# First expert pair's activations ahead of the place gates, residual rebuild behind them, in a one-core decoder layer

## The chip, the cores and the metric

The kernel runs on one core of one Trainium2 chip. The metric is the device time of one execution in microseconds (us); the profile is one execution taken by the hardware profiler. The engines are named as in the profile: PE (matmul), PEld (its weight loads), DVE (VectorE), ACT (ScalarE), POOL (GpSimd), SP (the queue that issues most loads).

## The reference

One decoder layer over 512 tokens of width 1024: a token mixer (sparse attention and a gated DeltaNet), a LayerNorm, and a hierarchical mixture of experts with a second LayerNorm. The change is in the last part. Cut to it:

```python
h = x * (1.0 + sc2) + sh2                      # 512 tokens x 1024
# each token: one of 4 groups, in it the top 2 of 8 experts, with gates
def expert_block(args):                        # 32 experts, FF = 512
    xb, e = args
    hb = jax.nn.silu(xb @ w_gate[e]) * (xb @ w_up[e])
    return hb @ w_down[e]
y = sum over a token's experts of gate * expert_block(token)
x = layer_norm(alpha * x + (1.0 + gt2) * y, ln_g[1], ln_b[1])
```

## The kernel before

The experts are worked in 16 pairs (`pair(p)`, `PAIRS = 16`), four experts to a group. A pair's tokens are gathered with one-hot matmuls into 2 x 64 places. PE then computes for the pair `pwg` (gate product) and `pwu` (up product), each as two halves of 16 matmuls (`first_product(p, "wg" or "wu", i)`, L1259). `expert_rows` (L1139) makes the activations: tanh on ACT (L1142), a multiply on DVE (L1143, both in a tile `eth` that has one buffer), and the product with `pwu` on DVE (L1145, tile `hb`). `turned_rows` (L1149) transposes `hb` on PE (L1153, `hbT`) and copies it on ACT (L1155, `hbTs`). `last_products` (L1271) multiplies by the down weights (`py`, L1279), and `weighted` (L1158) scales the result by the gate (DVE L1162, tile `ys` with two buffers) and splits it in two parts (ACT L1167, DVE L1168). One pair later `combine_block` (L1176) puts them back to token order (PE `comb`, L1184) and DVE adds them to the residual rows `acc` (L1190).

Which place holds which token and with what gate is worked out once per two pairs by `place_gates` (PE `gs` L1229, then ACT L1231, whose rows share the one-buffer tile `eth`) and `turned_gates` (PE `gsT` L1240, then small DVE steps L1243 and L1246 into `gsl`). `token_hots` (L1250, DVE L1253) makes the one-hot rows for `comb`; `tokens_of` (DVE L975) those for the gather of a later group.

Between the routing and pair 0 the residual rows `acc` are rebuilt from the two parts of the normed tokens: eight DVE additions (L1519), each 128 x 512, and behind each one POOL addition (L1527) of a bias row `b_row`, which POOL loads (L1522) and scales (L1523). `b_row` stands in the two `ys` buffers. The two halves of `acc` lie in memory that early loaded weights used (`acc0`, `acc1` in `EARLY`), so their rebuild waits for the matmuls that read these weights.

Each engine runs its instructions in one order that is fixed when the program is built: by the order of writing, by what is ready, and by explicit edges. `tc.issue_after(ins)` puts what its block issues on the engine of `ins` behind `ins`. `in_turn()` (L1299) chains PE's pieces of the pairs in this way. `begun` is the last matmul of pair 0's `pwu`; behind it come `gs` and `gsT`. In `whole(p)` (L1318) the call `rows_of(p)` stands ahead of the pair's remaining PE work.

Weights come as 1 MB loads on SP (L1108, `load`), in one chain, each into a slot that a matmul some 13 loads before has released. Ahead of pair 14 there is a loop over overflowing places (`overflow`, L1428), which all engines enter together.

Of the kernel before, what the change touches and what calls it, by code (L numbers as in the profile page):

```python
# [9 lines left out]
F32 = mybir.dt.float32  # L10
# [4 lines left out]
OP = mybir.AluOpType  # L15
# [65 lines left out]
def decoder_layer(ctx: ExitStack, tc: tile.TileContext, A, out, dbg=None):  # L81
    nc = tc.nc
    v, g, s, pe = nc.vector, nc.gpsimd, nc.scalar, nc.tensor
# [110 lines left out]
    for c in (slice(0, 512), slice(512, 1024)):  # L194
        o = pmm("c")
        pe.matmul(o, row1, crow[:, c], start=True, stop=True)
        th = dp.tile([P, S], F32, name="cth", tag="cacc", bufs=2)
# [77 lines left out]
    def project(n, i, rhs=None, name="pj", split=None, bank=None, first=0):  # L275

        hi, lo = split or take(n, i)
        o = (bank or pmm)(name)[:, first:]
        r = rhs or (h_hi, h_lo)
        for k in range(KT):  # L280
            mm3(o, (hi[:, k, :], lo[:, k, :]), (r[0][:, k, first:], r[1][:, k, first:]), k == 0, k == KT - 1)
        look_ahead()
        return o
# [56 lines left out]
    first = {i: project("w_in", i, split=early[i], bank=banks[i]) for i in range(6)}  # L340
# [130 lines left out]
    for h in range(H):  # L471
# [5 lines left out]
        for n in range(NT):  # L477
            v.scalar_tensor_tensor(NTm[:, h, n, :], o[:, n, :], per_head(brk2, n, h), et[:, n, :],
                                   op0=OP.mult, op1=OP.mult)
# [11 lines left out]
    for j in range(31):  # L491
        n, w = 31 - j, j + 1
# [40 lines left out]
    for j in range(4):  # L533
        o = project("w_in", T_QI + j, first=P)
        for b in range(2):
            r, x = slice(64 * b, 64 * b + 64), slice(64 - 64 * b, 128 - 64 * b)
            s.activation(q_st[b][r, j, :], o[r], AF.Copy)
            v.tensor_tensor(q_st[b][x, j, :], o[r], q_st[b][r, j, :].bitcast(F32), op=OP.subtract)
    for i in range(1, NT):
        N = (i + 1) * P  # L540
        sc = isc[i - 1]
        for h in range(H):
# [9 lines left out]
            else:  # L552
                v.scalar_tensor_tensor(sc[:, :N], rl[:, :N], widx[:, i, h:h + 1], sc[:, :N],
                                       op0=OP.mult, op1=OP.add)
# [73 lines left out]
    for h in range(H):  # L628
# [32 lines left out]
        for n in range(NT):  # L661
            v.scalar_tensor_tensor(qk[:, n, :], o[:, n, :], per_head(rk, n, h), et[:, n, :],
                                   op0=OP.mult, op1=OP.mult)
# [3 lines left out]
                                          op=OP.mult)  # L667
# [195 lines left out]
    for d in range(KT):  # L863
# [14 lines left out]
        for t in range(NT):  # L878
            x = part[0][:, t * P:(t + 1) * P]
# [138 lines left out]
    n = slice(0, 512)  # L1018
# [117 lines left out]
    load_ahead([seq[i] for i in FIRST])  # L1136


    def expert_rows(pg, pu, n):  # L1139

        th = mo.tile([P, FF], F32, name="eth", bufs=1)
        s.activation(th[:n], pg[:n], AF.Tanh, scale=0.5)  # L1142
        v.scalar_tensor_tensor(th[:n], th[:n], 1.0, pg[:n], op0=OP.add, op1=OP.mult)  # L1143
        hb = m2.tile([P, 4, P], F32, name="hb", bufs=1)
        v.scalar_tensor_tensor(hb[:n], th[:n].rearrange("s (p j) -> s j p", j=4), 0.5,  # L1145
                               pu[:n].rearrange("s (p j) -> s j p", j=4), op0=OP.mult, op1=OP.mult)
        return hb

    def turned_rows(hb, n, last=False):  # L1149

        o = pc("hbT", (P, 4, P))
        for j in range(4):
            pe.transpose(o[:, j, :n], hb[:n, j, :], ident[:n, :n])  # L1153
        hT = lp.tile([P, 4, P], F32, name="O") if last else m2.tile([P, 4, P], F32, name="hbTs")
        s.activation(hT[:, :, :n], o[:, :, :n], AF.Copy)  # L1155
        return hT
# [40 lines left out]
    def gather(O, n, xg, j, bank=pb):  # L1197
        o = bank("gx", (P, 2, 256))
        for i in range(2):
            for t in range(NT):  # L1200
                for q, hh in enumerate((n_hi, n_lo)):
                    pe.matmul(o[:, i, :n], hh[:, t, (j + i) * P:(j + i + 1) * P], O[:, t, :n],  # L1202
                              start=(t == 0 and q == 0), stop=(t == NT - 1 and q == 1))
        evacuate(xg, o, j, n, bank is pmm)
# [20 lines left out]
    def place_gates(gi, O):  # L1225

        o = pb("gs", (9, 2 * P))
        for t in range(NT):
            pe.matmul(o, gate_hl[:, t, gi], O[:, t, :], start=(t == 0), stop=(t == NT - 1))  # L1229
        rows = mo.tile([P, FF], F32, name="eth", bufs=1)[:9, :2 * P]  # L1230
        s.activation(rows, o, AF.Copy)  # L1231
        return rows

    def turned_gates(rows):


        o = pb("gsT", (P, 2, 9))
        r = []
        for c in range(2):
            pe.transpose(o[:, c, :], rows[:, c * P:c * P + P], ident[:9, :9])  # L1240
        for c in range(2):
            gs = mo.tile([P, 9], F32, name="gsl", bufs=4)
            v.scalar_tensor_tensor(gs[:, 1:], o[:, c, 8:9].to_broadcast([P, 8]), float(SLOTS), lim, op0=OP.add, op1=OP.subtract)  # L1243
            for x in range(2):
                p = slice(64 * x, 64 * x + 64)
                v.tensor_reduce(gs[p, 0:1], o[p, c, 4 * c + 2 * x:4 * c + 2 * x + 2], axis=X, op=OP.add)  # L1246
            r.append(gs)
        return r
# [5 lines left out]
                        gs_of[p][:, 1:, None].to_broadcast([P, 8, SLOTS]), op=OP.is_equal)  # L1254
        return OT

    groups, first, OTs, py_done = {}, {}, {}, [None]

    def first_product(p, nm, i):  # L1259

        if i == 0:
            first[p, nm] = pmm("p" + nm)
        o, xg, c0 = first[p, nm], groups[p // 2][1], p % 2 * P
        ws = [half(A["w_gate" if nm == "wg" else "w_up"], 2 * p + x, i, nm) for x in range(2)]
        for j in range(4):
            for x in range(2):
                done = pe.matmul(o[64 * x:64 * x + 64], xg[:, 4 * i + j, c0 + 64 * x:c0 + 64 * x + 64],  # L1267
                                 ws[x][:, j * FF:(j + 1) * FF], start=(i == 0 and j == 0), stop=(i == 1 and j == 3))
        return done
# [28 lines left out]
    @contextmanager  # L1298
    def in_turn():  # L1299

        with tc.issue_after(behind[0]) if behind[0] is not None else nullcontext():
            yield
        behind[0] = next(i for i in reversed(nc.cur_bb.bb.instructions) if i.engine == begun.ins.engine)

    def rows_of(p):
        return expert_rows(first.pop((p, "wg")), first.pop((p, "wu")), P)
# [3 lines left out]
    def combinations():  # L1310

        def step(parts, c, OT, t):
            return lambda: combine_block(parts, c, OT, P, t, pa if t % 2 else pb)
        steps = [step(*x, t) for x in waiting for t in range(NT)]
        waiting.clear()
        return steps

    def whole(p):  # L1318


        gi = p // 2
        hb = rows_of(p)
        nxt = groups.get(gi + 1)

        turned = []

        def gates():
            turned.append(place_gates(gi, groups[gi][0]))

        def turn_gates():  # L1330
            gs_of[p], gs_of[p + 1] = turned_gates(turned[0])

        js = () if nxt is None or p == 0 else (0, 2, 4, 6) if p == 1 else (4 * (p % 2), 4 * (p % 2) + 2)
        gathers = [lambda j=j: gather(nxt[0], 256, nxt[1], j, pmm) for j in js]
        combs = combinations()
        gates, turn_gates = ([gates], [turn_gates]) if gi and p % 2 == 0 else ([], [])
        steps = combs[:4] + gates + gathers[:1] + combs[4:] + turn_gates + gathers[1:]
        for f in steps:
            with in_turn():
                f()  # L1340
        with in_turn():
            return turned_rows(hb, P)

    def pair(p):

        gi, q = p // 2, p + 1
        if p == 0:
            with in_turn():
                first_product(q, "wg", 0)
        hT = whole(p)  # L1350
        if p % 2 == 1 and gi + 2 < E // 4 or p == 0:
            n = gi + 2 if p else 1
            groups[n] = tokens_of(n)
        OTs[p] = token_hots(p)
        with in_turn():
            if p:
                first_product(q, "wg", 0)
            first_product(q, "wg", 1)
        with in_turn():
            waiting.extend(y + (OTs[p],) for y in last_products(p, hT))  # L1360
        with in_turn():
            first_product(q, "wu", 0)
            first_product(q, "wu", 1)
# [57 lines left out]
    def overflow():  # L1421
# [6 lines left out]
        with tc.For_i(0, n_over, 1) as it:  # L1428
# [20 lines left out]
            for src in (A["w_gate"], A["w_up"]):  # L1449
                o = pa("pwx")  # L1450
                for i in range(2):
                    w_ = half_of(wx, src, e, i)
                    for j in range(4):
                        pe.matmul(o[:SLOTS], xg[:, 4 * i + j, :SLOTS], w_[:, j * FF:(j + 1) * FF],
                                  start=(i == 0 and j == 0), stop=(i == 1 and j == 3))
                pgu.append(o)
            hT = turned_rows(expert_rows(pgu[0], pgu[1], SLOTS), SLOTS)
            py = [pa("py") for _ in range(2)]
            for i in range(2):
# [48 lines left out]
    started = first_product(0, "wu", 0)  # L1508
    places, turn = m1.tile([P, 2048], F32R, name="places", tag="a0"), [1]
    begun = first_product(0, "wu", 1)  # L1510
    with tc.issue_after(begun.ins):
        gs_of[0], gs_of[1] = turned_gates(place_gates(0, groups[0][0]))

    acc = Parts(*[lp.tile([P, 2, D], F32, name="acc", tag=f"acc{i}", bufs=1) for i in range(2)])
    for c in range(2):
        for t in range(NT):
            x, hi, lo = (y[:, t, :].rearrange(f"q ({o}) -> q j p", j=KT)[:, :, 64 * c:64 * c + 64]
                         for y, o in ((acc, "p j"), (n_hi, "j p"), (n_lo, "j p")))
            v.tensor_tensor(x, hi.bitcast(F32), lo.bitcast(F32), op=OP.add)  # L1519
    b_row = [m2.tile([P, 512], F32, name="ys", bufs=2) for _ in range(2)]  # L1520
    for c in range(2):
        g.dma_start(b_row[c], A["ln"][0][1][c * 512:(c + 1) * 512][None].to_broadcast([P, 512]))  # L1522
# [1 line left out]
    for c in range(2):  # L1524
        for t in range(NT):
            x = acc[:, t, c * 512:(c + 1) * 512]
# [23 lines left out]
    with tc.issue_after(nm_done.ins):  # L1550
        x = acc[:, 0, :]
        s.activation(x, x, AF.Identity, bias=nm[:, 0:1], scale=rs[:, 0:1])
        for t in (1, 2, 3):
            x = acc[:, t, :]
# [4 lines left out]
        x = acc[:, 0, :]  # L1559
# [82 lines left out]
```

## Time and profile before

| | us |
|---|---|
| median of 3 runs | 1273.54 (1272.57 to 1275.81) |
| profiled execution, own time | 1277.16 |
| its span | 1275.5 |
| mean granted TensorE clock of the span | 0.976 |

The page gives the busy time of each engine, the span in 40 slices of 31.9 us with the granted clock (PEclk, tenths of full speed) and the load rate, the chain that ended last, and groups of instructions. A timeline row gives start, duration, engine, line, operation, out<-in and count; in brackets the engine's idle time before it and what ended it.

### The profile page before, as it was taken

The numbers are of one execution on the slowest core, as the hardware profiler recorded it, in microseconds if no ns is written. First come the engines' busy times: TensorE is split into PE (matmuls) and PEld (weight loads), VectorE is DVE, ScalarE is ACT, GpSimd is POOL, SyncE is SP. The second block draws the span as 40 slices with busy tenths as digits, with TensorE's granted clock in tenths as the row PEclk, the third lists the DMA queues.
The fourth block names the chain that finished last, engine by engine and source line by source line (L and its number), as shares of the span: only waits on it lengthen the run. The fifth ranks groups of instructions, "written<-read, shape, count | busy, mean of one in ns | idle before, by whom it ended". The sixth has DMA issues, their size and how long they took to land. (4 is left out here: it accounts for less than half of the span.)

```text
span 1275.5 us, 16286 instructions
## 1 busy us (share of the span) xinstructions
PE 1174.5 (92%) x6042; PEld 803.4 (63%) x6042; DVE 789.2 (62%) x1701; ACT 433.4 (34%) x913; POOL 230.7 (18%) x190
## 2 busy tenths in 40 slices
PE   4977988998899999999999978999999999999994
PEld 2766766777677777778888864454455555555432
DVE  6797898598995656866646876533324243333338
ACT  3454643666455656432223222111111111111102
POOL 4322234233232321000024232300000000000003
PEclk9999998999999999999999989899999999999987
DMA  7614314111211111356644777779999999999792
GB/s 276 254 67 131 109 50 139 56 49 48 67 49 35 67 67 67 128 208 240 248 149 182 291 281 274 292 323 420 422 420 422 421 421 420 421 420 421 318 386 110
DMA packets 75860, 292.37 MB, mean 229 GB/s; under 512 B 19169, under 2 KB 31617, under 8 KB 51202
## 3 DMA queue, kind: packets, MB, share of 16 engines
q1 hardware_dynamic: 58706, 282.47, 56.4%
q10 hardware_dynamic: 16352, 6.16, 2.0%
q0 software_dynamic: 720, 2.66, 0.6%
q8 instruction: 49, 0.80, 0.3%
q14 instruction: 33, 0.27, 0.1%
HBM read 287.57 MB, written 3.70 MB: 228 GB/s over the span
## 5 line engine op out<-in xcount | busy, mean ns | idle before, releaser
L228 PE MATMUL pj<-h_hi,w_hi 128*128 128x512 f32 (+1 forms) x504 | 203.3, 410 | 18.2 <-ACT h_hi L323 12.9
L230 PE MATMUL pj<-h_hi,w_lo 128*128 128x512 f32 (+1 forms) x504 | 204.9, 408 | 4.6 <-POOL w_lo L224 4.0
L229 PE MATMUL pj<-h_lo,w_hi 128*128 128x512 f32 (+1 forms) x504 | 204.9, 407 | 0.0
L224 POOL TENSOR_TENSOR w_lo<-wr,w_hi 128x1024 fp32r<-128x1024 f32 x43 | 108.8, 2534 | 209.2 <-ACT w_hi L223 170.8
L223 ACT ACTIVATE w_hi<-wr 128x1024 fp32r<-128x1024 f32 x85 | 89.7, 1057 | 136.5 <-PE pj L229 92.9
L228 PEld LDWEIGHTS pj<-h_hi,w_hi 128*128 128x128 f32 x504 | 97.2, 193 | 39.7 <-ACT h_hi L323 14.9
L1267 PE MATMUL pwg<-wg,xg 128*64 128x512 f32 x512 | 119.7, 615 | 0.0
L1267 PE MATMUL pwu<-wu,xg 128*64 128x512 f32 x512 | 115.2, 592 | 0.0
L230 PEld LDWEIGHTS pj<-h_hi,w_lo 128*128 128x128 f32 x504 | 97.2, 193 | 24.6 <-POOL w_lo L224 6.1
L229 PEld LDWEIGHTS pj<-h_lo,w_hi 128*128 128x128 f32 x504 | 97.3, 193 | 18.2 <-DVE h_lo L324 0.8
L1279 PE MATMUL py<-wd,hbTs 128*64 128x512 f32 x480 | 106.1, 593 | 0.0
L1267 PEld LDWEIGHTS pwu<-wu,xg 128*64 128x64 f32 x512 | 47.3, 137 | 62.3 <-issue 60.0
L1188 POOL TENSOR_TENSOR acc<-acc,ad 128x256 f32<-128x256 f32 x8 | 6.0, 775 | 442.9 <-PE comb L1184 439.8
L1190 DVE TENSOR_TENSOR acc<-acc,comb 128x512 f32<-128x512 f32 (+1 forms) x128 | 77.6, 663 | 12.8 <-PE comb L1184 12.3
L1143 DVE SCALAR_TENSOR_TENSOR eth<-eth,pwg 128x512 f32<-128x512 f32 x16 | 11.0, 688 | 115.3 <-ACT eth L1142 113.0
L1267 PEld LDWEIGHTS pwg<-wg,xg 128*64 128x64 f32 x512 | 37.9, 141 | 69.2 <-issue 66.7
L1279 PEld LDWEIGHTS py<-wd,hbTs 128*64 128x64 f32 x480 | 39.9, 137 | 63.6 <-issue 63.6
L1162 DVE SCALAR_TENSOR_TENSOR ys<-py,gsl,gt2r 128x512 f32<-128x512 f32 (+1 forms) x34 | 24.4, 718 | 83.2 <-PE py L1279 79.7
L224 DVE TENSOR_TENSOR w_lo<-wr,w_hi 128x1024 fp32r<-128x1024 f32 x42 | 56.8, 1354 | 29.6 <-ACT w_hi L223 28.8
L357 DVE SCALAR_TENSOR_TENSOR cacc<-pad,convw,cacc 128x512 f32<-128x512 f32 x72 | 68.4, 955 | 6.3 <-ACT cacc L355 6.1
L965 ACT ACTIVATE xg<-gx,h2c 128x256 f32<-128x256 f32 x32 | 17.9, 565 | 122.6 <-PE gx L1202 114.8
L1145 DVE SCALAR_TENSOR_TENSOR hb<-eth,pwu 128x512 f32<-128x512 f32 x16 | 17.2, 1077 | 65.8 <-PE pwu L1267 65.8
(476 smaller groups left out, 2340.3 us busy)
## 6 DMA issues: line engine op xcount, KB each, us to landing
wg<-in_w_gate_dram SPq DMA_DIRECT2D x64, 1024.0 KB, 11.7
wu<-in_w_up_dram SPq DMA_DIRECT2D x64, 1024.0 KB, 15.5
wd<-in_w_down_dram SPq DMA_DIRECT2D x60, 1024.0 KB, 12.0
wr<-in_w_in_dram SPq DMA_DIRECT2D x31, 1024.0 KB, 5.0
wada<-in_w_ada_dram SPq DMA_DIRECT2D x23, 1024.0 KB, 5.5
wr<-in_w_br_dram SPq DMA_DIRECT2D x8, 1024.0 KB, 6.4
gr<-g_rows ACTq DMA_DIRECT2D x16, 256.0 KB, 5.0
wr<-in_w_out_dram SPq DMA_DIRECT2D x4, 1024.0 KB, 5.0
```

The costliest lines, as they stand in the source:

```text
L223: s.activation(hi, raw, AF.Copy)
L224: (lo_eng.pop() if len(lo_eng) > 1 else lo_eng[0]).tensor_tensor(lo, raw, hi.bitcast(F32), op=OP.subtract)
L228: pe.matmul(o, a[0], b[0], start=start, stop=False)
L229: pe.matmul(o, a[0], b[1], start=False, stop=False)
L230: pe.matmul(o, a[1], b[0], start=False, stop=stop)
L357: v.scalar_tensor_tensor(acc, pad[:, i:i + S], convw[:, ct, i:i + 1], acc, op0=OP.mult, op1=OP.add)
L965: x = s.activation(xg[:, j, :n], o[:, 0, :n], AF.Identity, bias=h2c[:, 1, 1, j:j + 1], scale=h2c[:, 1, 0, j:j + 1])
L1145: v.scalar_tensor_tensor(hb[:n], th[:n].rearrange("s (p j) -> s j p", j=4), 0.5, pu[:n].rearrange("s (p j) -> s j p", j=4), op0=OP.mult, o ...
L1162: v.scalar_tensor_tensor(ys[:n, :w], py, gs, gt2r[:n, c], op0=OP.mult, op1=OP.mult)
L1190: v.tensor_tensor(acc[:, t, c], acc[:, t, c], o[:, :w], op=OP.add)
L1267: done = pe.matmul(o[64 * x:64 * x + 64], xg[:, 4 * i + j, c0 + 64 * x:c0 + 64 * x + 64], ws[x][:, j * FF:(j + 1) * FF], start=(i == 0 and ...
L1279: pe.matmul(py[c][64 * x:64 * x + 64], hT[:, 2 * i + j, 64 * x:64 * x + 64], ws[x][:, j, 512 * c:512 * c + 512], start=(i == 0 and j == 0) ...
```

## The change

`expert_rows` records its last DVE instruction (L1145) as `rows_done[0]`. Pair 0's `expert_rows` is called right behind `begun` and its result kept in `hidden[0]`, which `whole(0)` takes in place of a call of its own. The place gates of pairs 0 and 1 are then issued behind `begun` (on PE) and behind that L1145 (on DVE), and the eight DVE additions of the residual rebuild (L1519) behind the same L1145. No instruction is added or taken away.

```diff
+    rows_done = [None]
+
     def expert_rows(pg, pu, n):
         th = mo.tile([P, FF], F32, name="eth", bufs=1)
         s.activation(th[:n], pg[:n], AF.Tanh, scale=0.5)
         v.scalar_tensor_tensor(th[:n], th[:n], 1.0, pg[:n], op0=OP.add, op1=OP.mult)
         hb = m2.tile([P, 4, P], F32, name="hb", bufs=1)
-        v.scalar_tensor_tensor(hb[:n], th[:n].rearrange("s (p j) -> s j p", j=4), 0.5,
-                               pu[:n].rearrange("s (p j) -> s j p", j=4), op0=OP.mult, op1=OP.mult)
+        rows_done[0] = v.scalar_tensor_tensor(hb[:n], th[:n].rearrange("s (p j) -> s j p", j=4), 0.5,
+                                              pu[:n].rearrange("s (p j) -> s j p", j=4), op0=OP.mult, op1=OP.mult)
         return hb
...
-    groups, first, OTs, py_done = {}, {}, {}, [None]
+    groups, first, OTs, py_done, hidden = {}, {}, {}, [None], {}
...
         gi = p // 2
-        hb = rows_of(p)
+        hb = hidden.pop(p) if p in hidden else rows_of(p)
...
     begun = first_product(0, "wu", 1)
-    with tc.issue_after(begun.ins):
+    hidden[0] = rows_of(0)
+    with tc.issue_after(begun.ins), tc.issue_after(rows_done[0].ins):
         gs_of[0], gs_of[1] = turned_gates(place_gates(0, groups[0][0]))
...
-            v.tensor_tensor(x, hi.bitcast(F32), lo.bitcast(F32), op=OP.add)
+            with tc.issue_after(rows_done[0].ins):
+                v.tensor_tensor(x, hi.bitcast(F32), lo.bitcast(F32), op=OP.add)
```

## Rows read from the trace of the kernel before

**Rows 1.** From the page: the span, and the load rate in the 40 slices of 31.9 us.

```profile
span 1275.5 us, 16286 instructions
...
GB/s 276 254 67 131 109 50 139 56 49 48 67 49 35 67 67 67 128 208 240 248 149 182 291 281 274 292 323 420 422 420 422 421 421 420 421 420 421 318 386 110
```

**Rows 2.** The waits of PE from 790 us to the end: who waited for whom, us in total, times, longest.

```profile
PE hbT L1153 <- DVE hb L1145: 5.6, 1, 5.6
PE gsT L1240 <- ACT eth L1231: 3.2, 2, 2.8
PE gs L1229 <- DVEq L1428: 2.7, 1, 2.7
PE py L1289 <- ACT O L1155: 0.7, 1, 0.7
```

**Rows 3.** Timeline of PE around the stretch, to pair 1.

```profile
785.85 2.31 PE L1267 MATMUL pwg<-wg,xg 128*64 128x512 f32 x9
787.74 3.85 PE L1267 MATMUL pwu<-wu,xg 128*64 128x512 f32 x16
791.52 0.63 PE L1229 MATMUL gs<-O,gate_hl 128*9 128x256 f32 x4
792.61 0.29 PE L1240 MATMUL gsT<-ident,eth 9*128 9x9 f32 x2 [0.46 <-ACT eth L1231]
798.48 1.11 PE L1153 MATMUL hbT<-ident,hb 128*128 128x128 f32 x4 [5.58 <-DVE hb L1145]
799.53 5.87 PE L1267 MATMUL pwg<-wg,xg 128*64 128x512 f32 x16
805.23 7.03 PE L1279 MATMUL py<-wd,hbTs 128*64 128x512 f32 x32
812.10 7.03 PE L1267 MATMUL pwu<-wu,xg 128*64 128x512 f32 x32
...
819.24 0.50 PE L1184 MATMUL comb<-yh,places 128*128 128x512 f32 x1
```

**Rows 4.** Timeline of DVE, then of ACT, over the same stretch.

```profile
794.12 2.00 DVE L1519 TENSOR_TENSOR acc<-n_hi,n_lo 128x512 f32<-128x512 f32 x2
...
796.76 0.68 DVE L1253 TENSOR_TENSOR places<-slot_no,gsl 128x512 fp32r<-128x512 f32 x1
797.36 1.06 DVE L1145 SCALAR_TENSOR_TENSOR hb<-eth,pwu 128x512 f32<-128x512 f32 x1
798.34 2.06 DVE L975 TENSOR_TENSOR O<-slot_no,pos 128x256 fp32r<-128x256 f32 x4
...
811.52 1.65 DVE L1162 SCALAR_TENSOR_TENSOR ys<-py,gsl,gt2r 128x512 f32<-128x512 f32 x2 [4.73 <-PE py L1279]
...
819.21 1.07 DVE L1145 SCALAR_TENSOR_TENSOR hb<-eth,pwu 128x512 f32<-128x512 f32 x1 [4.65 <-PE pwu L1267]
...
792.19 0.37 ACT L1231 ACTIVATE eth<-gs 9x256 f32<-9x256 f32 x1 [12.40 <-PE gs L1229]
793.00 0.60 ACT L1142 ACTIVATE eth<-pwg 128x512 f32<-128x512 f32 x1 [0.44 <-PE gsT L1240]
```

**Rows 5.** PE after two other short idle times, and the granted clock (the figure behind the POOL column, 1.00 is full) in stretches behind them and in the stretch of the change.

```profile
748.53 0.19 PE L1004 MATMUL pos<-selb,upper_b 128*128 128x32 bf16 x1 [1.88 <-DVE selb L1002]
...
770.35 0.19 PE L1004 MATMUL pos<-selb,upper_b 128*128 128x32 bf16 x1 [1.38 <-DVE selb L1002]
...
750.00:752.00 2.00, 2.00 (x11) 2.00 (x11) 0.69 (x1) 0.00 (x0) 0.00 (x0) 0.50 0.81 340
...
772.00:774.00 2.00, 1.99 (x14) 1.15 (x14) 1.00 (x2) 1.02 (x2) 0.00 (x0) 1.00 0.86 360
...
798.00:800.00 2.00, 1.52 (x6) 1.01 (x8) 2.00 (x5) 0.37 (x1) 2.00 (x2) 0.50 0.00 0
...
804.00:806.00 2.00, 2.00 (x12) 0.65 (x10) 0.00 (x0) 0.53 (x1) 2.00 (x3) 0.99 0.03 8
```

**Rows 6.** Timeline of POOL, and the durations (ns, least/median/most) of the rebuild's additions and of one-hot rows for the gather.

```profile
795.37 1.97 POOL L1523 TENSOR_SCALAR ys<-ys 128x512 f32<-128x512 f32 x1 [2.37 <-DMA ys<-in_ln_dram]
797.43 1.27 POOL L1527 TENSOR_TENSOR acc<-acc,ys 128x512 f32<-128x512 f32 x1
798.66 1.67 POOL L1523 TENSOR_SCALAR ys<-ys 128x512 f32<-128x512 f32 x1
800.30 9.20 POOL L1527 TENSOR_TENSOR acc<-acc,ys 128x512 f32<-128x512 f32 x7
...
L1519 DVE TENSOR_TENSOR acc<-n_hi,n_lo x8: 1081/1093/1123, 786.6 to 795.0; 128x512 f32<-128x512 f32 x8
L1527 POOL TENSOR_TENSOR acc<-acc,ys x8: 1262/1272/1825, 797.4 to 808.2; 128x512 f32<-128x512 f32 x8
...
L975 DVE TENSOR_TENSOR places<-slot_no,pos x4: 417/423/425, 786.2 to 791.0; 128x256 fp32r<-128x256 f32 x4
```

**Rows 7.** The weight loads: SP's issues at 805 us, then the last four loads of `wu` ahead of the loop and the time from issue to landing of these four, and the PE row that uses them.

```profile
805.42 4.24 SPq L1108 DMA_DIRECT2D wd<-in_w_down_dram  x4
...
L1108 SPq DMA_DIRECT2D wu<-in_w_up_dram x4: 327/328/385, 1169.1 to 1176.3; - x4
...
DMA to landing us min/median/max: 19.0/19.6/19.8
...
1197.39 7.09 PE L1267 MATMUL pwu<-wu,xg 128*64 128x512 f32 x32
```

## The prediction

> **What bounds the kernel now.** I read the page first, for where the end is set; then PE's waits in the expert part, since PE has the most work there; then the timelines of PE, DVE, ACT and POOL around the edited lines; then the granted clock; last the loads. The load rate stands near 420 GB/s from slice 28 on [rows 1], so the weights are a candidate for the bound, but in the list of PE's waits from 790 us to the end no row names a DMA [rows 2]. There PE sets the pace, and only four waits are left. The longest, 5.6 us, is the one that the edit touches: pair 0's `hbT` waits for `hb` from DVE [rows 2].
>
> The reader is to see in the PE timeline that `pwu` of pair 0 ends at 787.74 + 3.85 = 791.59, that `gs` and `gsT` fill little, and that `hbT` starts only at 798.48 [rows 3]. The cause stands in the DVE and ACT rows: ACT may start the tanh only at 793.00, since `eth` has one buffer and holds the gate rows until `gsT` has read them; DVE does two rebuild additions from 794.12, then L1143, then one-hot rows (L1253) at 796.76, and only at 797.36 the product L1145 that PE waits for [rows 4]. A second cost follows: the granted clock is 0.50, the lower level of 1.2 GHz, from 798 to 804 us, and full again after it [rows 5], so `hbT` and 16 matmuls of `pwg` take from 798.48 to 805.23 [rows 3].
>
> **The change part by part.** *Activations first.* Nothing is added; the same tanh, multiply and product move up. The tanh needs only pair 0's `pwg`. The last row of `pwg` matmuls before the rest of `pwu` ends at 785.85 + 2.31 = 788.16, whichever product they belong to [rows 3]; tanh (0.60) and L1143 (0.7, taken as the 0.68 of the like-sized L1253) then end by 789.5 [rows 4], under the `pwu` matmuls that run to 791.59, and ACT had been idle 12.40 us there [rows 4]. Without that cover they would cost 1.3 us. So DVE has only L1145 left when `pwu` ends. In pair 1 it starts 0.08 us behind `pwu` (812.10 + 7.03 = 819.13 to 819.21) and takes 1.07 [rows 3, 4]: `hb` is there at 791.59 + 0.08 + 1.07 = 792.74. PE followed `hb` by 0.06 before (798.42 to 798.48) [rows 3, 4], so `hbT` can start at 792.80, 5.7 us earlier.
>
> *Gates behind it.* `gs` stays where it is on PE. Its ACT copy (0.37 [rows 4]) now waits for the one `eth` buffer, thus for L1145: 792.74 to 793.15, and `gsT` (0.29 [rows 3]) can go at 793.2. If PE's order has `hbT` first, `gsT` lies behind it and takes 0.29 off the gain: 5.4. If `gsT` stands first, `hbT` starts at 793.5: 5.0. I take 5.3. Queued behind the later gate rows are `gsl`, the one-hot rows and, by 804 us, the weighting of `py` on DVE; that has 10 us.
>
> *The clock.* PE's idle time becomes 0.65 us (from the end of `gs` at 792.15 to 792.80), or 1.05 with `gsT` first. Behind an idle time of 1.38 us the clock stayed full, behind one of 1.88 us it fell to 0.50 [rows 5]. The new one is below the shorter. At full clock 16 such matmuls take half of 812.10 - 805.23, 3.43, and `hbT` half of 1.05, 0.52, together 3.95 against the 6.75 before [rows 3]: 2.8 us more. The bounds are 0 (it falls anyway) and 2.8; by the nearest row I take 2.8.
>
> *The rebuild behind it.* Eight DVE additions of 1.09 us [rows 6], 8.7 us in all, now start at 792.74. DVE is done with them and with two L1253 (0.68 each [rows 4]) at about 803; the `py` that DVE has to weight next ends near 812.10 - 8.1 = 804.0. That hides them; the cover is thin, 1 us. POOL's chain (scale 1.97, add, scale 1.67, seven adds) ran from 795.37 to 809.50 behind the landing of its own bias rows [rows 6], not behind DVE, and its 1.27 us an add is slower than DVE's 1.09, so it should end near 809.5 again. But `b_row` holds the two `ys` buffers, so the second L1162 may start only then; that had been hidden by an L1162 at 811.52 [rows 4]. It now ends at 809.5 + 0.83 = 810.3, and PE comes to the first `comb` at 819.24 - 8.1 = 811.1 [rows 3]. The margin of 0.8 us also has to hold the split of `ys` and whatever POOL loses to a busier DVE. One POOL add of eight took 1.83 instead of 1.27, beside DVE additions; and four L975 took 2.06 beside POOL where four alone take 4 x 0.42 = 1.7 [rows 4, 6]. So some loss is likely. The bounds of what is given back are 0 and the 3.1 to 5.9 of the third rival; I take 0.5.
>
> The Trainium skill (SBUF — State Buffer, section Who interferes with whom) speaks against the change here: a DVE instruction with two SBUF inputs and a GpSimd instruction that reads SBUF shut each other out for the whole instruction. The trace agrees in part only: 1.83 and 2.06 are such delays, but the L1253 at 796.76 ran 0.68 us beside a POOL instruction, its ordinary time [rows 4, 6]. By the rule the sum would be that of the slower rival below; by the rows it is this one.
>
> *Sum.* 5.3 + 2.8 - 0.5 = 7.6 us. All that follows on PE moves up with it, loads too: SP's next loads, at 805.42, go out as the last of these `pwg` matmuls (799.53 + 5.87 = 805.40) frees their slots [rows 3, 7]. No queue of loads is passed. The profiled execution took 1277.16 us, so 1269.6; it was 3.6 us above the median of the runs, 1273.54, which becomes 1265.9.
>
> **The rivals.** *The clock falls anyway.* Gain 4.8, 1268.7. For it: 0.65 to 1.05 us of idle with short instructions around it; against it: the row at 1.38.
>
> *POOL becomes the next wait.* If the other seven adds also take 1.83, POOL ends 7 x 0.56 = 3.9 later, 813.4; the second L1162 ends at 814.2, and PE, ready for `comb` at 811.1, waits 3.1 us. That is over 1.88, so the clock may fall for another 2.8. Gain 8.1 - 3.1 = 5.0, or 2.2: 1268.5 to 1271.3, say 1270. For it: the one slow add and the 0.8 us margin; against it: six of eight at 1.27 [rows 6].
>
> *Slower: DVE and POOL take turns.* Behind `hb` stand eight L1519 (8.7), two L1253 (1.4) and four L975 (1.7), 11.8 us, and on POOL 1.97 + 1.67 + 8 x 1.27 = 13.8. If none of it overlaps, from 792.8 it ends at 818.4, both L1162 (1.65 [rows 4]) at 820.0: `comb` comes 0.8 us later than the 819.24 of before, behind an idle time of 9 us that costs 2.8 in clock: 1277.1. It decides from a chain end of 817.6 on. Against it: DVE worked nearly without a break from 795.4 to 800.4 beside POOL [rows 4, 6].
>
> *The weight stream does not move.* The last `wu` load ahead of the loop goes out at 1176.3 and lands at most 19.8 later, 1196.1; the second half of its product starts at 1197.39 + 3.43 = 1200.8 [rows 7]. The slack is 4.7, so a stream that stood still would give back 7.6 - 4.7 = 2.9: 1268.8, with a slower clock behind the wait 1271.6. Against it: the loads wait for PE, as shown.
>
> *The change doesn't do what it says.* DVE's or PE's order leaves something ahead of `hb` or `hbT` that waits as long: no gain, 1273.5. Only L975 can stand ahead on DVE, at 0.42 each.
>
> **How the numbers follow.** Forecast 0.62, clock 0.12, POOL 0.12, taking turns 0.06, stream 0.04, no effect 0.04. A measurement here tells apart about 0.3%, 3.8 us: faster is below 1269.7. The forecast, the clock, half of POOL and half of the stream lie there: 0.82. Slower, above 1277.4, holds most of the turns: 0.04. The rest, 0.14, is the same. The range runs from the full 8.1 with 2 us for the spread of runs, 1263.5, to 1270.5, past the POOL case; the forecast's own is 1264 to 1268.
>
> **What would show it.** Right: L1142 and L1143 before 790 us, L1145 within 0.1 us of the end of `pwu`, `hbT` near 793, a granted clock of 1.00 from 790 to 812 us, `comb` of pair 1 near 811.5 and the same distances from there to the end. Wrong: 0.50 behind `gs`; PE waiting in pair 1 at `comb` for DVE, with POOL's adds past 811; a wait of PE for `wu` near 1190; or DVE at other work when `pwu` ends.

## The result, and the profile after

The changed kernel takes 1286.76 us (median of 4 runs, 1283.92 to 1287.91); the kernel before, beside it on the same chip, takes 1274.67 (1272.57 to 1276.16). The ratio is 1.0097, with a 95% interval of 1.0079 to 1.0115: about 12 us slower, where 7.6 us faster was forecast. The profiled execution took 1287.91 us. Line numbers of after are 2 higher than before up to the overflow loop and some way behind it (L1428 is now L1430), and 4 higher from the rebuild on (L1519 is now L1523); the edits of the experiments shift some of theirs further.

From the page of after, the span:

```profile
span 1286.2 us, 16292 instructions
```

PE's waits from 775 us to the end of after, the list of [rows 2]:

```profile
PE gs L1231 <- DMA wu<-in_w_up_dram: 18.8, 1, 18.8
PE comb L1186 <- ACT yh L1169: 2.0, 1, 2.0
PE gsT L1242 <- ACT eth L1233: 1.6, 1, 1.6
...
PE comb L1186 <- DVE yl L1170: 0.7, 1, 0.7
PE hbT L1155 <- DVE hb L1147: 0.6, 1, 0.6
```

The 5.6 us of `hbT` has become 0.6. Two things are new: 2.7 us at `comb` of pair 1, and 18.8 us at the first `gs` behind the overflow loop, where before 2.7 us were waited for DVE [rows 2]. This one is on a load, and no load was waited for before.

**Where the edit stands.** Timeline of PE, the rows that answer to [rows 3]:

```profile
787.02 3.86 PE L1269 MATMUL pwu<-wu,xg 128*64 128x512 f32 x16
790.81 0.63 PE L1231 MATMUL gs<-O,gate_hl 128*9 128x256 f32 x4
792.04 0.66 PE L1155 MATMUL hbT<-ident,hb 128*128 128x128 f32 x4 [0.59 <-DVE hb L1147]
792.62 0.29 PE L1242 MATMUL gsT<-ident,eth 9*128 9x9 f32 x2
792.84 3.65 PE L1269 MATMUL pwg<-wg,xg 128*64 128x512 f32 x16
796.33 7.04 PE L1281 MATMUL py<-wd,hbTs 128*64 128x512 f32 x32
803.19 7.04 PE L1269 MATMUL pwu<-wu,xg 128*64 128x512 f32 x32
810.16 0.25 PE L1394 MATMUL cnt<-ones_b,selb 128*32 128x1 bf16 x4
812.37 0.50 PE L1186 MATMUL comb<-yh,places 128*128 128x512 f32 x1 [1.96 <-ACT yh L1169]
813.55 0.50 PE L1186 MATMUL comb<-yl,places 128*128 128x512 f32 x1 [0.69 <-DVE yl L1170]
```

Executions differ by some us in how early they come to this point, so I count from the start of `gs`, 790.81 here and 791.52 before. `py` starts 5.52 us behind it instead of 13.71: a gain of 8.2. `hbT` of pair 1 starts 35.8 us behind it instead of 39.4: 3.7 are left (differences are taken before rounding), so 4.5 are given back at `comb`. Up to `hbT` of pair 13 that hardly changes (387.8 for 391.6). Across the loop, to `hbT` of pair 14, after takes 47.1 us where before takes 31.8: 15.3 lost. From there to the end it is 60.5 for 60.6. So -3.7 + 15.3 - 0.1 = +11.5 us from `gs` to the end (495.4 for 483.9).

**The give-back.** DVE, then POOL, in the same stretch of after; [rows 4, 6] hold the same instructions before:

```profile
790.92 1.06 DVE L1147 SCALAR_TENSOR_TENSOR hb<-eth,pwu 128x512 f32<-128x512 f32 x1 [3.98 <-PE pwu L1269]
...
794.60 7.52 DVE L1523 TENSOR_TENSOR acc<-n_hi,n_lo 128x512 f32<-128x512 f32 x6
801.96 1.71 DVE L1255 TENSOR_TENSOR places<-slot_no,gsl 128x512 fp32r<-128x512 f32 x1
...
804.28 5.03 DVE L975 TENSOR_TENSOR O<-slot_no,pos 128x256 fp32r<-128x256 f32 x4
809.24 1.75 DVE L1255 TENSOR_TENSOR places<-slot_no,gsl 128x512 fp32r<-128x512 f32 x1
...
812.15 0.75 DVE L1164 SCALAR_TENSOR_TENSOR ys<-py,gsl,gt2r 128x512 f32<-128x512 f32 x1 [0.50 <-POOL acc L1531]
...
797.00 1.93 POOL L1531 TENSOR_TENSOR acc<-acc,ys 128x512 f32<-128x512 f32 x1
798.89 2.22 POOL L1527 TENSOR_SCALAR ys<-ys 128x512 f32<-128x512 f32 x1
801.08 11.04 POOL L1531 TENSOR_TENSOR acc<-acc,ys 128x512 f32<-128x512 f32 x7
```

POOL's seven adds take 11.04 us instead of 9.20 and end at 812.12; the second L1164, which needs the buffer that they hold, starts at 812.15. POOL's first add takes 1.93 us for 1.27 and its second scaling 2.22 for 1.67; with the seven adds that is 3.1 of the 3.3 us by which the chain ends later, counted from `gs` (21.3 us behind it for 18.0). PE had been ready for `comb` at 810.41. Up to there the granted clock was full; behind the two short waits it falls once more (the figure behind the POOL column, as in [rows 5]):

```profile
790.00:812.00 22.00, 19.82 (x99) 6.71 (x94) 20.63 (x23) 1.88 (x4) 18.29 (x12) 1.00 0.81 322
815.00:818.20 3.20, 3.20 (x15) 2.95 (x13) 3.05 (x9) 0.00 (x0) 0.00 (x0) 0.50 1.01 420
```

**The loss.** A row of the chain that ended last, at the loop, then SP's own waits from 1180 to 1240 us, then its issues, all of after:

```profile
1202.24 19.75 DMA wu<-in_w_up_dram
```

```profile
SPq L1430 <- SPq L1430: 13.8, 4, 6.3
...
SPq L1430 <- DMA wu<-in_w_up_dram: 3.7, 2, 2.3
```

```profile
1186.70 6.77 SPq L1108 DMA_DIRECT2D wd<-in_w_down_dram  x4
1194.80 7.77 SPq L1108 DMA_DIRECT2D wu<-in_w_up_dram  x4
1222.75 16.48 SPq L1108 DMA_DIRECT2D wd<-in_w_down_dram  x8
```

and SP's issues before, of the same eight loads:

```profile
1210.76 1.99 SPq L1108 DMA_DIRECT2D wd<-in_w_down_dram  x4
1212.79 1.98 SPq L1108 DMA_DIRECT2D wu<-in_w_up_dram  x4
```

The last eight of the twelve 1 MB loads that `overflow()` issues ahead (four `wd` of pair 14, four `wu` of pair 15) went out behind the loop before, and go out ahead of it now. The last of them is issued at 1202.24 and lands 19.75 us later; so long SP stands at the loop's line, and PE, done with its last `comb` at 1204.0, with it. The reads of the loop's count (`nx`) by SP show the same change of order, first before, then after:

```profile
L1427 SPq TENSOR_LOAD <-nx x1: 467/467/467, 824.0 to 824.0; - x1
```

```profile
L1429 SPq TENSOR_LOAD <-nx x1: 481/481/481, 1202.6 to 1202.6; - x1
```

The diff touches neither this read nor the loads. The order in which a queue gets its instructions is worked out anew when the program is built, and it came out differently some 400 us behind the edit.

### The profile page after: what moved, and what is told of

Read it like the earlier page. It is cut to its first block, busy times and chain, and to the rows that moved or that the text cites. A ratio compares the mean times of both kernels' runs of the same rounds, so it can differ in the third digit from the quotient of the medians.

```text
span 1286.2 us, 16292 instructions
## 1 busy us (share of the span) xinstructions
PE 1177.2 (92%) x6042; PEld 806.0 (63%) x6042; DVE 795.6 (62%) x1701; ACT 432.8 (34%) x913; POOL 234.0 (18%) x190
## 4 chain that ended last, share of the span: by engine, by line
PE 70%; DVE 16%; ACT 3%; DMA 3%; POOL 3%; issue 3%; ACTq 0%; DVEq 0%; POOLq 0%; SPq 0%
PE pwg L1269 9%; PE pwu L1269 8%; PE py L1281 8%; PE pj L230 7%; PE pj L228 7%; PE pj L229 7%; PE comb L1186 5%; PE gx L1204 4%; DVE cacc L357 2%; DMA wu<-in_w_up_dram 2%; DMA gr<-g_rows 1%; POOL acc L1531 1%; POOL w_lo L224 1%; PE pt L791 1%; PE po L230 1%
## 5 line engine op out<-in xcount | busy, mean ns | idle before, releaser
L228 PE MATMUL pj<-h_hi,w_hi 128*128 128x512 f32 (+1 forms) x504 | 204.1, 411 | 15.5 <-ACT h_hi L323 10.9
L1145 DVE SCALAR_TENSOR_TENSOR eth<-eth,pwg 128x512 f32<-128x512 f32 x16 | 11.0, 688 | 126.0 <-ACT eth L1144 125.9
L1164 DVE SCALAR_TENSOR_TENSOR ys<-py,gsl,gt2r 128x512 f32<-128x512 f32 (+1 forms) x34 | 24.4, 718 | 78.8 <-PE py L1281 74.9
L1169 ACT ACTIVATE yh<-ys 128x512 fp32r<-128x512 f32 (+1 forms) x33 | 20.1, 610 | 114.3 <-DVE ys L1164 114.3
```

Of the source, the lines that this page charges most:

```text
L228: pe.matmul(o, a[0], b[0], start=start, stop=False)
L1164: v.scalar_tensor_tensor(ys[:n, :w], py, gs, gt2r[:n, c], op0=OP.mult, op1=OP.mult)
```

## The experiments

Ratios are to the kernel before on the same chip. "From `gs`" is worked out from each profiled execution: its span less the start of the gate product `gs` of pair 0. The last two columns are PE's waits.

| kernel | us, median | ratio, 95% interval | from `gs` to the end | at the loop | at `comb` of pair 1 |
|---|---|---|---|---|---|
| before | 1274.7 | | 483.9 | 2.7 | none |
| after | 1286.8 | 1.0097 [1.0079, 1.0115] | 495.4 | 18.8 | 2.7 |
| x1 | 1271.3 | 0.9976 [0.9963, 0.9989] | 480.4 | 2.6 | 2.7 |
| x2 | 1290.1 | 1.0120 [1.0100, 1.0140] | 498.5 | 18.6 | none |
| x3 | 1268.0 | 0.9950 [0.9931, 0.9970] | 475.6 | 2.7 | none |
| x4 | 1273.1 | 0.9986 [0.9970, 1.0002] | 481.7 | 2.7 | 1.5 |
| x5 | 1267.6 | 0.9950 [0.9933, 0.9967] | 476.1 | 2.6 | none |
| x6 | 1267.0 | 0.9942 [0.9925, 0.9959] | 475.9 | 2.7 | none |
| x7 | 1277.0 | 1.0017 [0.9995, 1.0039] | 485.7 | 9.8 | 2.7 |
| x8 | 1270.8 | 0.9974 [0.9956, 0.9991] | 480.5 | 2.6 | 2.7 |
| x9 | 1267.5 | 0.9941 [0.9926, 0.9955] | 475.7 | 2.7 | none |
| x10 | 1283.1 | 1.0079 [1.0064, 1.0094] | 491.2 | 18.5 | none |

**x1, the loads put back behind the loop.**

```diff
-        load_ahead([(nm, 2 * q + x, i) for nm, q, i in seq for x in range(2)][:len(AGAIN) - 1])
+        todo = [(nm, 2 * q + x, i) for nm, q, i in seq for x in range(2)][:len(AGAIN) - 1]
+        load_ahead(todo[:4])
+        held = [slot(nm) for nm, e, i in todo[4:]]
...
+        for t, (nm, e, i) in zip(held, todo[4:]):
+            load(t, A[{"wg": "w_gate", "wu": "w_up", "wd": "w_down"}[nm]][e][:, i * 2048:(i + 1) * 2048])
+            ahead[nm, e, i] = t
```

> The changed kernel, with one thing more: the last eight 1 MB loads ahead of the overflow loop (down weights of pair 14, up weights of pair 15) are issued behind the loop, as in the kernel before. Theory A (the time was lost on SP: with these loads ahead of the loop, SP's entry into the loop waits until all of them have landed, 18.8 us of idle PE at gs against 2.7 before): PE's wait at the loop goes back to about 2.7 us, and the time to 1286.8 - 16.1 + 1.1 (their landing is no longer done when the loop ends) = 1271.8, between 1270 and 1273. Rival B (the loads as a stream are late, whatever their place): PE waits for them behind the loop instead, 1283 or more.

Measured: 1271.3. The wait on the load is gone, the waits at `comb` stay. The two rows of PE's waits in x1:

```profile
PE gs L1231 <- DVEq L1432: 2.6, 1, 2.6
PE comb L1186 <- ACT yh L1169: 2.0, 1, 2.0
```

So 15.5 us of the loss are the order of these loads, and the change in itself gains 3.4. SP's read of the count still stands right ahead of the loop in x1 (at 1183.0 us), so a late read alone costs nothing that shows; it is the loads ahead of the loop that cost.

**x2, the same order put into the kernel before.** The read of the count is tied behind the last weight load (`loads[-1]`), and the eight loads fall ahead of the loop.

```diff
-        n_over = nc.values_load(
+        with tc.issue_after(loads[-1].ins):
+          n_over = nc.values_load(
```

> The kernel before, with SP's read of the loop count tied behind the last load, which puts the same eight loads ahead of the loop; nothing else is changed. Theory A: before, the last load ahead of the loop landed at 1206.0 us of the span; eight more at 2.49 us each land by 1225.9, so the loop is entered at about 1226 instead of 1210, and with 1.1 us won back behind it the time is 1274.7 + 14.6 = 1289.3 (1286 to 1291). Rival B: the order on SP does not matter, 1274.7.

Measured: 1290.1, with PE's longest wait as in after:

```profile
PE gs L1229 <- DMA wu<-in_w_up_dram: 18.6, 1, 18.6
```

The price (15.3 us over before) does not need the edit at all.

**x7, half the dose.** As x1, with `todo[:8]` ahead and `todo[8:]` behind.

> The changed kernel with four instead of eight of the last 1 MB loads ahead of the overflow loop. Theory A (the loop is entered when every load in flight has landed, one each 2.49 us): TensorE's wait at the loop falls from 18.8 us by four times 2.49 us to about 8.9 us, and the time lies about 9 us under the changed kernel's 1286.8, near 1277.5. Theory B (something else of the change makes the 12 us, the number of loads does not matter): near 1286.8 or near x1's 1271.3, not between.

Measured: 1277.0, 9.8 us below after. PE's wait (this list names no load as its end, but the rows of `wd` name PE's `gs` as waiting 9.8 us for them) and SP's issues:

```profile
PE gs L1231 <- issue: 9.8, 1, 9.8
```

```profile
1188.31 6.77 SPq L1108 DMA_DIRECT2D wd<-in_w_down_dram  x4
1215.20 2.10 SPq L1108 DMA_DIRECT2D wu<-in_w_up_dram  x4
```

Eight loads cost 18.8 us, four 9.8: 2.25 us a load, near the 2.49 us that 1 MB takes at the 421 GB/s of [rows 1] (an estimate). What sets the wait is when the last load ahead of the loop lands: at 1222.0 in after and at 1214.2 in x7, and `gs` starts 0.8 and 1.2 us behind that. Each load put ahead of the loop moves this landing.

**x8, only the place of the count's read.**

```diff
             xe, xb, nx = overflow_list()
+            n_over = nc.values_load(nx[0:1, 0:1], min_val=0, max_val=OVER)
...
-        n_over = nc.values_load(nx[0:1, 0:1], min_val=0, max_val=OVER)
```

> The changed kernel with one statement moved: the read of the overflow loop's count stands right behind the making of the list that it counts, as early in SyncE's program as in the kernel before; with it the eight loads fall behind the loop again. If it is that order alone, and not the early hidden rows, that costs the 12 us: as x1, 1271.3, with a wait of about 2.6 us on the vector engine at the loop in place of 18.8 us. If the early read holds SyncE or TensorE up by itself (it waits for the list, some 4 us in the kernel before): up to 4 us more, 1275. If the order does not matter: 1286.8.

Measured: 1270.8, as x1. SP's read of the count and its next issues of the eight loads in x8:

```profile
L1541 SPq TENSOR_LOAD <-nx x1: 467/467/467, 815.7 to 815.7; - x1
```

```profile
1202.47 1.96 SPq L1108 DMA_DIRECT2D wd<-in_w_down_dram  x4
1204.47 2.01 SPq L1108 DMA_DIRECT2D wu<-in_w_up_dram  x4
```

Moving one statement by hand restores the order, with no cost of its own that shows.

**x3, the give-back: GpSimd's bias additions left out.** This kernel is x1 without the eight additions of the bias row, which leaves the bias out of the result; it is no candidate, and shows what they cost.

```diff
             x = acc[:, t, c * 512:(c + 1) * 512]
-            g.tensor_tensor(x, x, b_row[c], op=OP.add)
+            pass
```

> As x1, and POOL's eight additions of the bias row to the residual rows are left out (this part of the computation is missing). Theory C (the 4.5 us that PE loses at pair 1's comb come from DVE and POOL holding each other up over the rebuild: four L975 took 5.0 us instead of 1.7): without the adds DVE's queue runs at its own pace, pair 1's comb starts without a wait, and the time is 4 to 4.5 us below x1, about 1267.5. Rival D (DVE's queue alone is too long behind hb): the wait at comb stays and the time is that of x1.

Measured: 1268.0. DVE's instructions in x3:

```profile
792.87 6.51 DVE L1528 TENSOR_TENSOR acc<-n_hi,n_lo 128x512 f32<-128x512 f32 x6
799.23 0.67 DVE L1255 TENSOR_TENSOR places<-slot_no,gsl 128x512 fp32r<-128x512 f32 x1
...
800.51 1.43 DVE L975 TENSOR_TENSOR O<-slot_no,pos 128x256 fp32r<-128x256 f32 x4
```

In after the same rows take 7.52, 1.71 and 5.03. No wait at `comb` is left, and `hbT` of pair 1 stands 31.2 us behind `gs`, 8.2 earlier than before: the whole gain arrives. The four one-hot rows of after one by one (ns, least/median/most):

```profile
L975 DVE TENSOR_TENSOR O<-slot_no,pos x4: 794/1488/1493, 804.3 to 807.8; 128x256 fp32r<-128x256 f32 x4
```

The Trainium skill (SBUF — State Buffer, section Who interferes with whom) says that a DVE instruction with two SBUF inputs and a GpSimd instruction that reads SBUF shut each other out. The one-hot rows agree: three of the four take 1.49 us each, where one takes 0.42 with POOL idle [rows 6], and the POOL adds beside them take 1.45 for 1.27. The rebuild additions agree too. Seven of the eight take 1.09 to 1.46 us in after, as all eight do in x3, where POOL still scales its bias rows; the one that starts beside POOL's first add, at 797.76, takes 2.13. Where the addition starts first (801.02, 1.10 us), the add beside it takes longer (801.08, 2.04 us).

**x4, the one-hot rows of pair 1 moved behind the split of `ys`.** x1 with the four L975 and the L1255 of pair 1 issued behind L1170, which `split_done` records, so that DVE weights `py` first.

```diff
-            groups[n] = tokens_of(n)
-        OTs[p] = token_hots(p)
+            with tc.issue_after(split_done[0].ins) if p == 1 else nullcontext():
+                groups[n] = tokens_of(n)
+        with tc.issue_after(split_done[0].ins) if p == 1 else nullcontext():
+            OTs[p] = token_hots(p)
```

> As x1, and the one-hot rows that DVE makes in pair 1 (four L975 and one L1255) stand behind pair 0's weighting and its split (L1164, L1170) in DVE's order. Theory C with the queue order as its second half: the first L1164 no longer waits for 6.8 us of one-hot rows and starts near 804 instead of 810.9; the second still waits for POOL's last add (812 before, some 1 to 2 us earlier with fewer collisions), so the wait at comb falls from 2.7 to about 1 and the time to 1268.5 to 1270. If POOL's chain through the two ys buffers sets it alone: 1271.8 as x1.

Measured: 1273.1, by the medians 1.8 us over x1 (the two intervals overlap; counted from `gs` it is 1.3). DVE's two L1164 and PE's two waits in x4:

```profile
806.83 0.75 DVE L1164 SCALAR_TENSOR_TENSOR ys<-py,gsl,gt2r 128x512 f32<-128x512 f32 x1 [1.68 <-POOL acc L1538]
811.75 0.75 DVE L1164 SCALAR_TENSOR_TENSOR ys<-py,gsl,gt2r 128x512 f32<-128x512 f32 x1 [4.17 <-POOL acc L1538]
```

```profile
PE cnt L1406 <- DVE yl L1404: 2.6, 1, 2.6
...
PE comb L1186 <- DVE yl L1170: 1.5, 1, 1.5
```

DVE stood free and waited for POOL: it is POOL's chain through the two `ys` buffers that sets `comb`. And the one-hot rows now stood in front of the overflow list, for 2.6 us. My main expectation was wrong; the second one held in its mechanism (POOL's chain sets it alone).

**x5, four of the eight rebuild additions not held; x6, none held.** Both with the loads as in x1. x6 is the first part of the change alone.

```diff
-            with tc.issue_after(rows_done[0].ins):
+            with tc.issue_after(rows_done[0].ins) if t > 1 else nullcontext():
                 v.tensor_tensor(x, hi.bitcast(F32), lo.bitcast(F32), op=OP.add)
```

> The changed kernel with the last eight 1 MB loads behind the overflow loop (as x1), and only four of the eight rebuild additions held behind pair 0's hidden rows; the other four run under pair 0's wu product, where the vector engine stood idle for 3.97 us. Theory C (what the 1271.3 of x1 still gives back is the vector engine's rebuild and one-hot rows running beside GpSimd's eight bias additions): four additions of 1.0 us leave that stretch, the wait of 2.0 us at pair 1's combination and the half clock behind it go, hbT of pair 0 stays where it is in x1: 1268.0 to 1269.5, near x3's 1268.0. Theory D (GpSimd's own chain through the two buffers of its bias rows sets pair 1's combination, as in x4): the chain still starts only when its row has landed, so the wait stays and the time is x1's 1271.3.

> The changed kernel with the last eight loads behind the overflow loop (as x1), and no rebuild addition held: the first part of the change alone, with the order of the vector engine left to the scheduler. It puts five rebuild additions ahead of pair 0's hidden rows, so these should come about 1.0 us later than in x1 (hbT about 2.2 us behind the start of the gate product instead of 1.2), and behind them the stretch is five additions shorter. Theory C: 1269 to 1270.5, between x5 and x1. Theory that the second part (holding all eight) is needed: over 1271.3, nearer to the kernel before.

Measured: 1267.6 and 1267.0, which is no difference between them; both lie under the bounds that I gave (1268.0 and 1269). DVE and POOL in x5, then PE's wait for `hb` in x6:

```profile
786.60 3.90 DVE L1528 TENSOR_TENSOR acc<-n_hi,n_lo 128x512 f32<-128x512 f32 x4
...
791.67 1.06 DVE L1147 SCALAR_TENSOR_TENSOR hb<-eth,pwu 128x512 f32<-128x512 f32 x1 [0.25 <-PE pwu L1269]
...
798.15 2.90 DVE L975 TENSOR_TENSOR O<-slot_no,pos 128x256 fp32r<-128x256 f32 x4
...
800.96 9.09 POOL L1536 TENSOR_TENSOR acc<-acc,ys 128x512 f32<-128x512 f32 x7
```

```profile
PE hbT L1155 <- DVE hb L1147: 1.3, 1, 1.3
```

Four additions fit under `pwu`, in time in which DVE stood idle for 3.98 us in after; then POOL's seven adds take 9.09 again and end at 810.05, which is 18.5 us behind `gs` (21.3 in after). In x6 a fifth addition holds `hb` up by 0.7 us (1.3 of wait for 0.6), which costs less than the spread of the runs. Holding the rebuild behind the hidden rows, the second part of the change, costs 4.3 us (x1 against x6; 4.5 counted from `gs`).

**x9 and x10, the first part with and without the read moved.** x9 is x6 with the statement of x8 in place of the held loads; x10 is x6 with nothing done about the loads.

> The first part of the change alone (pair 0's hidden rows early, no rebuild addition held), with the one statement of x8 that reads the loop's count early. If the two findings add up: x6's 1267.0, that is 1266.0 to 1268.0, with no wait of TensorE on a load and none at pair 1's combination. If the early read costs something that x8's own waits hid: up to 1270.

> The first part of the change alone, with nothing done about the loads. If the early hidden rows alone make the scheduler put the eight loads ahead of the overflow loop, and their price does not depend on the rest: the changed kernel's 1286.8 less the 4.3 us by which x6 lies under x1, 1282.5, with TensorE's wait at the loop near 18.8 us. If only the held rebuild moved the loads: 1267.0, as x6.

Measured: 1267.5 and 1283.1. The findings add up: x9 beats before by 7 us and after by 19, with two edits of a few lines. And the first part of the change alone (hidden rows early, gates behind them) is enough to turn the order of the loads.

## Why the prediction was wrong, step by step

- **Activations first, gates behind: right.** The tanh and the multiply of pair 0 are done by 782.6 us, under the products; `hb` starts 0.1 us behind the gate product's start, `hbT` 1.23 behind it (forecast 1.28), `gsT` stands behind `hbT` as taken.
- **The clock: right.** It stays full behind the 0.59 us of idle time; 16 matmuls of `pwg` take 3.65 instead of the 5.87 of [rows 3]. Together 8.2 us at `py`, against the 8.1 of the sum.
- **The give-back: the mechanism named, the term mis-sized.** The sum had 0.5; it is 4.5, of which 2.7 is the wait and most of the rest the clock behind it. This is the rival "POOL becomes the next wait" (3.1 of wait, up to 2.8 of clock). The step that failed is "it should end near 809.5 again": counted from `gs`, the chain ended 21.3 us behind it, where before it was 18.0. Holding the additions put them and the one-hot rows beside POOL's adds. x4 shows that POOL's chain sets `comb`, x3 that without the adds DVE runs faster and no wait is left, and x5 that with four additions out of the way the chain ends 18.5 us behind `gs`. Two readings hid it. The one slow POOL add of before (1.83) was put down to DVE additions, but these had ended at 796.1, ahead of POOL's first add at 797.43 [rows 4, 6]; it started at 800.30, beside a one-hot row (L1253) that started at 800.32. So no row of before has a rebuild addition beside an add (and seven adds of the eight took 1.27, not six). And the cover of 1 us for DVE left out the four L975 (1.7) that also stand ahead of the first weighting, which started only at 810.91. A cover of 0.8 us was the warning. The rival "DVE and POOL take turns" went too far: it put the end of the chain 26.9 us behind `gs`, and the 12 us of loss do not come from it.
- **"No queue of loads is passed": false, and the sign hangs on it.** This is the step that turned a gain into a loss. "All that follows on PE moves up with it, loads too" was argued from one issue at 805 us. The argument took SP's order behind the edit for granted; eight loads passed the loop's entry, for 15.3 us. No rival had it: "the weight stream does not move" asked whether loads come too late, not whether more of them stand ahead of a place that waits for all. The trace of before showed half of it, SP at the loop while eight loads were still to come.
- **What would have been.** With the loads in their place the change gives 1271.3 (x1), 0.8 beyond the range; with the second part left out also, 1267.0 (x6), inside the forecast's own 1264 to 1268, though that is not the change that was forecast.

**Open.** Why the build puts SP's read of the count behind the last load once the hidden rows come early: no trace shows its reasons; x8 and x10 show only what turns it. And no general size for what DVE and POOL take from each other is worked out: four L975 took 2.06 us before [rows 4], where POOL was scaling a bias row during most of it [rows 6], 2.90 in x5, where one of the four ran beside an add (1.49 us), and 5.03 in after, all beside adds.

## What to carry to other kernels

Ahead of a time for an edit, list for each queue which instructions stand ahead of every loop or branch, and compare that list after the edit: it can change hundreds of microseconds away from the lines touched, and each 1 MB load put ahead of this loop cost about 2 us of PE's time (18.8 us of wait with eight, 9.8 with four). Read a loop's count right behind the making of it, so that its place does not hang on the scheduler. Work that is pushed behind a critical product lands beside something else; put as much of it as fits into the idle time under that product, and take a cover of less than a microsecond as none.

## What the runs showed of the hardware that I had not expected

- Entry into the loop on the count waits on SP until every load issued ahead of it has landed, though no row of its body stands in the trace: PE stands for 9.8 us with four of the eight loads ahead and for 18.8 with eight; with none its 2.6 us end with DVE, not with a load. The rows of SP at the loop's line are semaphore instructions of the program (19 of them in after), so this is how the loop is built; that the chip asks for it is not shown.
- A DVE instruction with two inputs in SBUF and a POOL add that run beside each other take longer, the one that starts second most of all: 1.49 us for a one-hot row that takes 0.42 with POOL idle, 1.71 to 1.75 for one that takes 0.67, 2.13 for a rebuild addition that takes 1.1, and 1.45 to 2.04 for a POOL add that takes 1.27.
